# Where matmul operands lie in SBUF: three small constants in one tile, and a 368-byte filler

## The chip, the cores and the metric

The kernel runs on one core of a Trainium2 chip, as one launch. The metric is device time in microseconds, from the start of an execution to its end. Before the change the median of three runs is 2976.22 us (2974.38 to 2978.99). Five engines matter here: TensorE (PE in the profile; its weight loads are shown apart as PEld), VectorE (DVE), ScalarE (ACT), GpSimd (POOL), and SyncE (SP), whose queue issues the DMAs.

## The reference, cut to what matters

The reference takes `x` of 512 tokens by 1024 features through two stacks of two layers. All arithmetic is fp32.

- First stack, layer 0: RMS norm, dilated sliding-window attention (3 groups of 8 heads, head dimension 128, windows 128, 512, 2048 with dilations 1, 4, 16, a bias from a table of 32 buckets), output projection, norm, residual. Then a feed-forward with a causal convolution of width 3: `u = conv(h @ W_up)`, `(gelu(u[:, :3072]) * u[:, 3072:]) @ W_down`.
- First stack, layer 1: a gated linear recurrence (input projection, convolution of width 4, two block-diagonal gates, a scan over the tokens, output projection), then the same feed-forward.
- Second stack, two layers: three attentions side by side on one input projection (differential attention with a bias table, stick-breaking attention, latent attention with rotary positions), an output projection, attention over a memory of 256 rows, and a feed-forward `square(relu(h @ W1)) @ W2` of 4096.

Nearly all of the work is products of a 512 x 1024 activation with weights:

```
h = rms_norm(x, g)                 # 512 x 1024
u = h @ w_up                       # 1024 x 6144, feed-forward of the first stack
y = act(u) @ w_down                # 3072 x 1024
u = h @ w_ff1; y = relu(u)**2 @ w_ff2   # 1024 x 4096, 4096 x 1024, second stack
```

## The kernel before, in words

*Products in three terms.* Each fp32 operand of a large product is held as two fp32r tiles, high part and rest. `mm3` (lines 159 to 163) adds three TensorE products into one accumulator in PSUM: high by high (L161), high by rest (L162), rest by high (L163):

```
mm(out, sh, mh, start=first, stop=False)
mm(out, sh, ml, start=False, stop=False)
mm(out, sl, mh, start=False, stop=last)
```

The first operand (`sh`, `sl`) is the stationary one, 128 x 128, which a weight load brings into the array; the second (`mh`, `ml`) is the moving one, 128 x 512 in most cases.

*Which tile is which operand.* `up` (L253) computes 128 output features for all 512 tokens: the weight tile `w` is stationary, the transposed activation `hT` moves; 8 steps over the 1024 features make 24 products. `down` and `down_last` (L515 to L556) compute 128 tokens by 512 output features: an activation tile (`act`, in other stages `oT`, `gh`, `mo`) is stationary, `w` moves. `proj_tok` (L891) and the value projections of the first attention compute tokens by features too, with `hT` stationary and `w` moving; a part of the latter reads `hT` with a stride of four tokens. The recurrence's gates have `w` stationary and `xh` moving.

*Weights.* `load` (L138) brings 512 KB by DMA into one of three `raw` tiles. `cut` (L144) writes the high part on ACT (L148) and the rest on DVE (L149) into one of five `w` tiles of the pool `ws`; in `down_last` the second half of the columns takes its `w` tiles from a pool of the stage's own. Inside `w`, high part and rest lie 4096 bytes apart, steps of a product 512 bytes (stationary) or 2048 bytes (moving). Inside `hT` high part and rest lie 16384 bytes apart, and the steps are 2048 bytes.

*Order.* The program is unrolled. Stages follow one another in `build` (L1559): first attention, feed-forward, recurrence, feed-forward, then for each of two layers the mixed attentions, the memory attention and a feed-forward. Within a stage, generators are woven by hand (`weave`, `pipe`, the lists `START`, `UNITS`, `FILL`); Tile, the layer that the kernel is written in, gives each engine its order of instructions and all semaphores, and assigns SBUF addresses.

*Places.* SBUF pools lie one behind the other in the order in which they are opened; a tile's bytes per partition are rounded up to a multiple of 32. The constants come first, from byte 16512 (the bytes below hold a DMA buffer of 16384 bytes and four constants of 32 bytes each). Worked out from the sizes, the tiles of the kernel before begin here:

```
tile or pool                       first byte    modulo 512
ident (512 bytes)                       16512           128
ones (4 -> 32)                          17024           128
x (16384)                               17056           160
hT (32768)                              33440           160
eps (4 -> 32), mhalf (32)               66208           160, 192
raws (3 x 4096)                         66272           224
ws (5 x 8192)                           78560           224
nrm (5 x 4096)                         119520           224
tiny (4224 in all)                     140000           224
pool "lruc" (768), later pool "two"    144224           352
first attention, first feed-forward,
  recurrence: oT, act, xh, gh          144992            96
second feed-forward and second stack:
  act (behind "two", 6688 bytes)       150912           384
```

`lruc` (L1572) holds the recurrence's small vectors and is closed after stage 2; `two` (L1582) then takes its place and holds the bias table `tb2` of 32 bytes, a mask, the rotary table and the memory's keys and values. Tiles of the pools opened later in a stage (the `w` tiles of `down_last`, for one) follow from there: 96 in the recurrence, 352 in the first feed-forward, 128 in the second, 384 in the last two.

*The small tiles.* `ones`, `eps` and `mhalf` are written once by POOL (L108, L112, L114); `mhalf` is read by the power that makes each norm's factor (L202, on POOL), `eps` by a logarithm on ACT, `ones` by a scan on DVE. `tb` (L312) and `tb2` (L823) hold the two bias tables; each is filled by one DMA and read as stationary operand in `toeplitz` (L285). `tiny` holds the small per-token statistics, four buffers of each kind.

Of the kernel before, what the change touches and what calls it, by code (L numbers as in the profile page):

```python
# [9 lines left out]
F32 = mybir.dt.float32  # L10
# [10 lines left out]
P = 128  # L21
NT = S // P
KD = D // P
NEG = -1e30
EPS = 1e-6


def hbm(ap, offset, dims):
# [3 lines left out]
def pipe(gens):  # L32

    live = []
    for g in gens:
        if g is not None:
            live.append(g)
        live = [x for x in live if next(x, 0) is None]
        yield
    while live:  # L40
        live = [x for x in live if next(x, 0) is None]
        yield
# [30 lines left out]
def weave(*streams):  # L73
    for _ in woven(*streams):
        pass
# [17 lines left out]
class Net:  # L93
    def __init__(self, ctx, tc, a):
        self.ctx, self.tc, self.nc, self.a = ctx, tc, tc.nc, a
        nc = tc.nc
        pool = lambda name, bufs, **k: ctx.enter_context(tc.tile_pool(name=name, bufs=bufs, **k))
        self.const = pool("const", 1)
        self.raws = pool("raws", 3)
        self.ws = pool("ws", 5)  # L100
        self.nrm = pool("nrm", 2)
        self.tiny = pool("tiny", 4)
        self.ps = pool("ps", 8, space=PSUM)
        self.dram = pool("dram", 1, space=DRAM)
        self.ident = self.const.tile([P, P], F32, name="ident")
        make_identity(nc, self.ident)
        self.ones = self.const.tile([P, 1], F32, name="ones")
        nc.gpsimd.memset(self.ones, 1.0)  # L108
        self.x = self.const.tile([P, NT, D], F32, name="x")
        self.hT = self.const.tile([P, 2, KD, S], F32R, name="hT")  # L110
        self.eps = self.const.tile([P, 1], F32, name="eps")
        nc.gpsimd.memset(self.eps, EPS)  # L112
        self.mhalf = self.const.tile([P, 8], F32, name="mhalf")
        nc.gpsimd.memset(self.mhalf, -0.5)  # L114
        self.lnexp = False
        self.stage = 0
        self.act_norm = False
        self.n = 0
        self.last_gelu = None
# [56 lines left out]
    def rsqrt(self, ss, scale, shape, tag):  # L176
# [4 lines left out]
        if shape[0] <= (1 if self.lnexp else 4):  # L181
            nc.vector.tensor_scalar(v, ss, scale, EPS, op0=ALU.mult, op1=ALU.add)
            nc.gpsimd.tensor_tensor(y, v, self.mhalf[:, :shape[0]], op=ALU.pow)
        else:
            nc.scalar.activation(v, ss, AF.Ln, bias=self.eps, scale=scale)
            nc.vector.tensor_scalar(nm, ss, -0.5 * scale, -0.5 * EPS, op0=ALU.mult, op1=ALU.add)
            nc.scalar.activation(y, v, AF.Exp, scale=-0.5)
# [5 lines left out]
    def rms(self, hs, n=D):  # L193
# [4 lines left out]
        for i, h in enumerate(hs):  # L198
            nc.scalar.activation(scr[:, i * n // 2:(i + 1) * n // 2], h, AF.Square, scale=n ** -0.5,
                                 accum_out=ss[:, i:i + 1])  # L200
        nc.vector.tensor_scalar(ss[:, 2:3], ss[:, 0:1], ss[:, 1:2], EPS, op0=ALU.add, op1=ALU.add)
        nc.gpsimd.tensor_tensor(ss[:, 3:4], ss[:, 2:3], self.mhalf[:, :1], op=ALU.pow)  # L202
# [92 lines left out]
    def attn(self, l):  # L295
# [4 lines left out]
        with ExitStack() as cx:  # L300
            qks = cx.enter_context(self.tc.tile_pool(name="at_qk", bufs=4))
            oTs = cx.enter_context(self.tc.tile_pool(name="at_o", bufs=8))
            one = cx.enter_context(self.tc.tile_pool(name="at_c", bufs=1))
# [5 lines left out]
            LS = (383, 255, 255)  # L309

            def setup():
                tb = one.tile([33, 24], F32, name="tb")  # L312
                nc.sync.dma_start(tb[:32], a["rel_bias"])
                nc.vector.memset(tb[32:33], NEG)
                for g in range(3):
                    oh = self.nrm.tile([P, D], F32, tag=("gb", "xn", "xn")[g], name=self.nm("oh"))[:33, :LS[g]]
                    nc.sync.dma_start(oh, a[f"c_oh{g}"])
                    if g == 0:
                        yield
                    scr.append(self.dram.tile([P, 8, LS[g]], F32, name=f"tz{g}"))  # L320
                    yield from self.toeplitz(lambda h, g=g: tb[:, g * 8 + h:g * 8 + h + 1], oh, LS[g], 8, scr[g],
                                             (lambda: self.nrm.tile([P, D], F32, tag="scr", name=self.nm("fz"), bufs=1))
                                             if g else (lambda: qks.tile([P, D], F32, tag="qk", name=self.nm("fz"))),
                                             None if g else self.bank)
# [217 lines left out]

            self.act_norm = False
            tables = setup()
            start()
            self.act_norm = True
# [271 lines left out]
    def setup2(self, pool):  # L818

        a, nc = self.a, self.nc  # L820
        L = 639
        self.da_scr = self.dram.tile([P, 8, L], F32, name="da_scr")
        tb = pool.tile([32, 8], F32, name="tb2")  # L823
        nc.sync.dma_start(tb, a["rel_bias_2"])
        oh = self.nrm.tile([P, D], F32, tag="xn", name=self.nm("oh"))[:32, :L]
        nc.sync.dma_start(oh, a["c_ohda"])
        yield from self.toeplitz(lambda h: tb[:, h:h + 1], oh, L, 8, self.da_scr,
                                 lambda: self.nrm.tile([P, D], F32, tag="scr", name=self.nm("fz"), bufs=1))
        self.cmask = pool.tile([P, 512], F32, name="cmask")
        nc.gpsimd.memset(self.cmask, 0.0)  # L830
        nc.gpsimd.memset(self.cmask[0:64, 448:], NEG)
        self.rope = pool.tile([P, NT, 2, 16], F32, name="rope")
        nc.sync.dma_start(self.rope, a["c_rope"].rearrange("(t p) c f -> p t c f", p=P))
# [725 lines left out]
def build(tc, a, out, stages=range(10)):  # L1559
    gains = ["norm_mix_pre", "norm_ffn_pre"] * 2 + ["mix_norm_g_2", "memx_norm_g_2", "ffn_norm_g_2"] * 2  # L1560
    layer = [0, 0, 1, 1, 0, 0, 0, 1, 1, 1]
    with ExitStack() as ctx:
        net = Net(ctx, tc, a)
        net.out = out[0]
        net.next_g, net.next_gb = a[gains[stages[0]]][layer[stages[0]]], None
        if stages[0]:
            for t in range(NT):
                tc.nc.sync.dma_start(net.x[:, t], a["x"][0, t * P:(t + 1) * P])
            weave((pipe(net.after(t) for t in range(NT)), 1))
        two = None  # L1570
        early = ExitStack()
        lru_pool = early.enter_context(tc.tile_pool(name="lruc", bufs=1))  # L1572
        for n, s in enumerate(stages):
            net.gains = [a[gains[i]][layer[i]] for i in stages[n + 1:n + 3]] + [None, None]
            net.next_g, net.next_gb = net.gains[0], None
            l = layer[s]
            net.stage = s
            net.act_norm = s < 2
            if s > 2:
                early.close()  # L1580
            if s in (3, 6) or s > 3 and two is None:
                two = two or ctx.enter_context(tc.tile_pool(name="two", bufs=1))  # L1582
                fill = net.prep(0 if s < 6 else 1, two)
            if s in (4, 7):
                weave((fill, 1))
                if not net.lnexp:
                    net.lnexp_tables()
            if s == 0:
                net.attn(l)
            elif s == 2:  # L1590
                if not hasattr(net, "lru_c"):
                    weave((net.lru_setup(lru_pool), 1))
                net.lru(l)
            elif s < 4:
                net.ffn1(l, fill if s == 3 else net.lru_setup(lru_pool))
            elif s in (4, 7):
                net.mix(l)
            elif s in (6, 9):
                net.ffn2(l, fill if s == 6 else None)
        early.close()  # L1600
# [64 lines left out]
```

## Time and profile before

```
median of three runs                       2976.22 us
profiled execution                         2979.35 us
its span, first to last instruction        2977.6 us
granted TensorE clock, mean                0.998
PE busy / PEld busy                        2927.2 us (98%) / 2402.7 us (81%)
DVE / ACT / POOL busy                      1676.8 us (56%) / 1250.8 us (42%) / 169.3 us (6%)
TensorE products                           14210
DMA                                        287.35 MB, mean 97 GB/s
```

How to read it: busy time is the union of an engine's instructions. Matmuls are pipelined, and each one's end is modelled, so that it overlaps the start of the next; a PE that is busy all the time can still be shortened. What one product costs in a full stream is the distance from its start to the next one's, which the view in order of time shows (start in us, length in us, engine, line, operation, tiles). Names stand as out<-in, the inputs in alphabetical order and not in the order stationary, moving.

### The profile page before, as it was taken

Reading aid. Unit: us, or ns where it says so; the run is one execution under the profiler, and the core shown is the slowest. Engines: PE = TensorE matmul, PEld = TensorE weight load, DVE = VectorE, ACT = ScalarE, POOL = GpSimd, SP = SyncE. Lnnn points to the kernel's source line nnn. Section 1 sums busy time; section 2 is a strip of 40 time slices with the busy share of each in tenths; the row PEclk is TensorE's granted clock in tenths of the full one; section 3 lists DMA queues with packets and bytes.
Section 4 is the critical chain, followed back from the end, with each engine's and each line's share of the span. In section 5 each row is a group of like instructions: output and inputs, shape, how many; then the busy total and the mean of one; then the engine's idle time right before and its main releaser. Section 6 shows DMA issues by size and latency. Waiting matters only on the chain.

```text
span 2977.6 us, 37084 instructions
## 1 busy us (share of the span) xinstructions
PE 2927.2 (98%) x14210; PEld 2402.7 (81%) x14210; DVE 1676.8 (56%) x3182; ACT 1250.8 (42%) x2427; POOL 169.3 (6%) x257
## 2 busy tenths in 40 slices
PE   9999999999999999999999999999999999999999
PEld 6888888888888778777887877888887877888887
DVE  3234344646556876445558587745545578754443
ACT  4333333543334664433345467523223467532221
POOL 0000000000000311000002031000001022000000
PEclk9999999999999999999999999999999999999999
DMA  5332232323332232333343331233333332123322
GB/s 183 95 87 84 80 93 96 110 93 94 97 92 85 78 121 88 95 107 112 95 121 108 107 123 43 66 105 113 109 92 115 101 123 79 29 85 96 96 93 71
DMA packets 335924, 287.35 MB, mean 97 GB/s; under 512 B 14041, under 2 KB 272484, under 8 KB 335748
## 3 DMA queue, kind: packets, MB, share of 16 engines
q1 hardware_dynamic: 335748, 284.99, 31.2%
q8 instruction: 112, 1.84, 0.3%
q14 instruction: 64, 0.52, 0.1%
HBM read 272.34 MB, written 12.62 MB: 96 GB/s over the span
## 4 chain that ended last, share of the span: by engine, by line
PE 55%; DVE 7%; ACT 2%; issue 1%; POOL 1%; DMA 1%; POOLq 0%; ACTq 0%; DVEq 0%
PE acc L161 16%; PE acc L162 16%; PE acc L163 16%; PE acc L1073 1%; PE tr L212 1%; PE acc L1086 1%; DMA raw<-in_w_in_dram 1%; PE tr L928 1%; DVE w L149 1%; PE acc L1218 1%; PE acc L1412 0%; ACT w L148 0%; PE acc L1392 0%; DVE z L1130 0%; DVE lru_hs L773 0%
## 5 line engine op out<-in xcount | busy, mean ns | idle before, releaser
L149 DVE TENSOR_TENSOR w<-raw,w 128x1024 fp32r<-128x1024 f32 (+1 forms) x456 | 553.3, 1216 | 388.9 <-ACT w L148 386.6
L161 PE MATMUL acc<-hT,w 128*128 128x512 f32 (+1 forms) x1992 | 761.2, 383 | 0.2 <-ACT hT L167 0.2
L163 PE MATMUL acc<-hT,w 128*128 128x512 f32 (+1 forms) x1992 | 758.4, 381 | 2.9 <-DVE w L149 2.8
L162 PE MATMUL acc<-hT,w 128*128 128x512 f32 (+1 forms) x1992 | 759.0, 381 | 0.4 <-DVE hT L168 0.4
L148 ACT CAST w<-raw 128x1024 fp32r<-128x1024 f32 (+2 forms) x464 | 477.8, 1033 | 497.7 <-PE acc L163 426.7
L163 PEld LDWEIGHTS acc<-hT,w 128*128 128x128 f32 x1992 | 375.0, 188 | 82.8 <-DVE w L149 4.2
L161 PEld LDWEIGHTS acc<-hT,w 128*128 128x128 f32 x1992 | 374.7, 188 | 81.2 <-issue 2.6
L162 PEld LDWEIGHTS acc<-hT,w 128*128 128x128 f32 x1992 | 375.0, 188 | 78.9 <-DVE hT L168 1.1
L162 PE MATMUL acc<-w,act 128*128 128x512 f32 x896 | 355.8, 397 | 0.0
L161 PE MATMUL acc<-w,act 128*128 128x512 f32 x896 | 354.1, 396 | 0.3 <-ACT act L167 0.3
L163 PE MATMUL acc<-w,act 128*128 128x512 f32 x896 | 352.4, 394 | 0.0
L161 PE MATMUL acc<-w,hT 128*128 128x512 f32 (+2 forms) x768 | 286.2, 373 | 1.3 <-ACT w L148 1.3
L163 PE MATMUL acc<-w,hT 128*128 128x512 f32 (+2 forms) x768 | 276.2, 360 | 0.0
L162 PE MATMUL acc<-w,hT 128*128 128x512 f32 (+2 forms) x768 | 275.2, 358 | 0.0
L587 DVE SCALAR_TENSOR_TENSOR u<-acc,cw,u 128x511 f32<-128x511 f32 x192 | 143.6, 748 | 205.9 <-ACT u L585 202.7
L161 PEld LDWEIGHTS acc<-w,act 128*128 128x128 f32 x896 | 168.3, 188 | 43.2 <-ACT act L167 1.6
L163 PEld LDWEIGHTS acc<-w,act 128*128 128x128 f32 x896 | 168.3, 188 | 40.3 <-DVE act L168 0.6
L162 PEld LDWEIGHTS acc<-w,act 128*128 128x128 f32 x896 | 168.4, 188 | 38.9
L161 PEld LDWEIGHTS acc<-w,hT 128*128 128x128 f32 x768 | 161.4, 210 | 21.4 <-issue 2.4
L162 PEld LDWEIGHTS acc<-w,hT 128*128 128x128 f32 x768 | 161.7, 211 | 17.1 <-issue 2.4
L163 PEld LDWEIGHTS acc<-w,hT 128*128 128x128 f32 x768 | 161.3, 210 | 15.1
L585 ACT ACTIVATE u<-acc,cw 128x512 f32<-128x512 f32 x96 | 74.6, 777 | 219.8 <-PE acc L163 219.7
(381 smaller groups left out, 3312.2 us busy)
## 6 DMA issues: line engine op xcount, KB each, us to landing
raw<-in_w_ff_dram SPq DMA_DIRECT2D x128, 512.0 KB
raw<-in_ffn_w_up_dram SPq DMA_DIRECT2D x96, 512.0 KB
raw<-in_attn_w_qkv_dram SPq DMA_DIRECT2D x72, 512.0 KB
raw<-in_ffn_w_down_dram SPq DMA_DIRECT2D x48, 512.0 KB
raw<-in_w_in_dram SPq DMA_DIRECT2D x40, 512.0 KB
raw<-in_lru_w_in_dram SPq DMA_DIRECT2D x16, 512.0 KB
raw<-in_w_out_dram SPq DMA_DIRECT2D x16, 512.0 KB
x<-in_x_dram SPq DMA_DIRECT2D x8, 512.0 KB
```

Of the source, the lines that this page charges most:

```text
L148: nc.scalar.copy(w[:, 0], raw)
L149: (lo or nc.vector).tensor_sub(w[:, 1], raw, w[:, 0].bitcast(F32))
L161: mm(out, sh, mh, start=first, stop=False)
L162: mm(out, sh, ml, start=False, stop=False)
L163: mm(out, sl, mh, start=False, stop=last)
L212: nc.tensor.transpose(b[:, j * P:(j + 1) * P], src[:, k * P:(k + 1) * P], self.ident)
L585: nc.scalar.activation(u, b, AF.Identity, bias=cw[:, 3, j:j + 1], scale=cw[:, 2, j:j + 1])
L587: nc.vector.scalar_tensor_tensor(u[:, s:], b[:, :S - s], cw[:, i, j:j + 1], u[:, s:], op0=ALU.mult, op1=ALU.add)
L928: nc.tensor.transpose(b[:, j * P:(j + 1) * P], src[:, j * P:(j + 1) * P], self.ident)
L1073: nc.tensor.matmul(o[:, oc:oc + dv], pT[:, k * P:(k + 1) * P], v(k), start=(k == 0), stop=(k == i))
L1086: nc.tensor.matmul(b[:, :w], QZ[:, h, m, i * P:(i + 1) * P], kT[:, h, :w], start=True, stop=True)
L1218: nc.tensor.matmul(b[:, :w], MT[:96, i, 0, h], MT[:96, :i + 1, 1, h], start=True, stop=True)
```

## The change

`ones`, `eps` and `mhalf` become columns 0, 1 and 2 to 9 of one tile `small` of 128 columns (512 bytes), which lies between `ident` and `x`. The bias tables `tb` and `tb2` become columns 32 to 55 and 16 to 23 of `small`, and leave the pools `at_c` and `two`. A tile `place` of 368 bytes that no instruction uses is taken from `tiny`. No engine instruction is added or removed.

```diff
+TINY = 368
...
+        self.small = self.const.tile([P, P], F32, name="small")
+        self.ones, self.eps, self.mhalf = self.small[:, 0:1], self.small[:, 1:2], self.small[:, 2:10]
-        self.ones = self.const.tile([P, 1], F32, name="ones")
         nc.gpsimd.memset(self.ones, 1.0)
         self.x = self.const.tile([P, NT, D], F32, name="x")
         self.hT = self.const.tile([P, 2, KD, S], F32R, name="hT")
-        self.eps = self.const.tile([P, 1], F32, name="eps")
         nc.gpsimd.memset(self.eps, EPS)
-        self.mhalf = self.const.tile([P, 8], F32, name="mhalf")
         nc.gpsimd.memset(self.mhalf, -0.5)
...
-                tb = one.tile([33, 24], F32, name="tb")
+                tb = self.small[:33, 32:56]
...
-        tb = pool.tile([32, 8], F32, name="tb2")
+        tb = self.small[:32, 16:24]
...
+        net.tiny.tile([P, TINY // 4], F32, name="place", bufs=1)
         lru_pool = early.enter_context(tc.tile_pool(name="lruc", bufs=1))
```

## Rows read from the trace of the kernel before

**Rows 1.** Stretches: from:to, length, busy us (count) of PE, PEld, DVE, ACT, POOL; clock, DMA.
```profile
587.00:946.00 359.00, 359.00 (x1549) 288.86 (x1548) 202.47 (x284) 131.44 (x164) 0.00 (x0) 1.00 0.32 99
992.00:1150.00 158.00, 148.10 (x624) 117.39 (x623) 124.28 (x151) 101.66 (x154) 40.19 (x37) 0.97 0.30 89
```

**Rows 2.** PE groups by line and shape: count, busy us, mean ns, idle before.
```profile
L161 PE MATMUL acc<-hT,w 128*128 128x512 f32 x1720 | 686.4, 399 | 0.0
...
L161 PE MATMUL acc<-w,act 128*128 128x512 f32 x896 | 354.1, 396 | 0.3 <-ACT act L167 0.3
...
L161 PE MATMUL acc<-w,hT 128*128 128x512 f32 x512 | 210.0, 410 | 0.0
...
L161 PE MATMUL acc<-hT,w 128*128 128x256 f32 x272 | 75.1, 280 | 0.2 <-ACT hT L167 0.2
L161 PE MATMUL acc<-w,hT 128*128 128x256 f32 x192 | 55.6, 289 | 1.3 <-ACT w L148 1.3
```

**Rows 3.** PE in order of time (start us, length us), `up`, first and 28th start.
```profile
599.77 0.39 PE L161 MATMUL acc<-hT,w 128*128 128x512 f32 x1
...
606.07 0.40 PE L161 MATMUL acc<-hT,w 128*128 128x512 f32 x1
```

**Rows 4.** The same, `down` of the second feed-forward, first and 25th start.
```profile
1212.07 0.40 PE L161 MATMUL acc<-w,act 128*128 128x512 f32 x1
...
1217.67 0.40 PE L161 MATMUL acc<-w,act 128*128 128x512 f32 x1
```

**Rows 5.** The same, `down` of the first feed-forward, first and 28th start.
```profile
627.75 0.40 PE L161 MATMUL acc<-w,act 128*128 128x512 f32 x1
...
634.01 0.40 PE L161 MATMUL acc<-w,act 128*128 128x512 f32 x1
```

**Rows 6.** The same, token projection of the mixed attentions, first and tenth start.
```profile
1610.40 0.39 PE L161 MATMUL acc<-w,hT 128*128 128x512 f32 x1
...
1612.46 0.40 PE L161 MATMUL acc<-w,hT 128*128 128x512 f32 x1
```

**Rows 7.** The same, recurrence's `down_last`: twelve with `ws`, twelve with own weights.
```profile
1123.17 0.39 PE L161 MATMUL acc<-w,gh 128*128 128x512 f32 x1
...
1125.73 0.40 PE L163 MATMUL acc<-w,gh 128*128 128x512 f32 x1
...
1127.12 0.39 PE L163 MATMUL acc<-w,gh 128*128 128x512 f32 x1
...
1128.48 0.39 PE L163 MATMUL acc<-w,gh 128*128 128x512 f32 x1
```

**Rows 8.** The same, products of the memory's keys, sixth and last of twelve.
```profile
1481.54 0.39 PE L163 MATMUL acc<-w,mT 128*128 128x512 f32 x1
...
1482.90 0.39 PE L163 MATMUL acc<-w,mT 128*128 128x512 f32 x1
```

**Rows 9.** The same, second feed-forward's `down_last`, own weights, six starts apart.
```profile
1568.70 0.39 PE L163 MATMUL acc<-w,act 128*128 128x512 f32 x1
...
1570.06 0.39 PE L163 MATMUL acc<-w,act 128*128 128x512 f32 x1
```

**Rows 10.** The same, first attention, `hT` stationary with a stride, 18 starts apart.
```profile
93.28 0.41 PE L161 MATMUL acc<-w,hT 128*128 128x512 f32 x1
...
97.60 0.41 PE L161 MATMUL acc<-w,hT 128*128 128x512 f32 x1
```

**Rows 11.** ACT groups in 600 to 940 us, then in 1210 to 1550 us.
```profile
L585 ACT ACTIVATE u<-acc,cw 128x512 f32<-128x512 f32 x40 | 31.1, 777 | 86.7 <-PE acc L163 86.7
...
L585 ACT ACTIVATE u<-acc,cw 128x512 f32<-128x512 f32 x37 | 28.8, 778 | 105.7 <-PE acc L163 105.7
```

**Rows 12.** Start of the kernel in order of time, and a row of SP's waits.
```profile
0.80 0.39 SPq L313 DMA_DIRECT2D tb<-in_rel_bias_dram  x1
0.86 0.08 DVE L314 MEMSET tb<- 1x24 f32 x1 [0.86 <-PEq L1652]
...
SPq L824 <- PE acc L163: 22.4, 1, 22.4
```

## The prediction

> **What bounds the kernel now.** Read the table of stretches first: in the first feed-forward (587 to 946 us, one of four such stages) TensorE is busy in all 359 us, DVE in 202, and the DMA engines for a third of the time; even in the recurrent stage, where DVE has most to do, TensorE holds 148 of 158 us [rows 1]. So the end is set by how fast TensorE gets through its queue. Next come the groups by line and shape: the 128x512 products of the three lines of `mm3` (L161, L162, L163) are 3 x 1720 with `hT` moving and `w` stationary, 3 x 896 with `w` moving and `act` stationary, 3 x 512 with `w` moving and `hT` stationary [rows 2]. Their "mean ns" of about 399 overlaps the next instruction and is no price; what counts is the distance from start to start, and only the order of time shows it.
>
> That distance depends on where the two operands lie, and this is what the change touches. I took each product's two addresses modulo 512 from the tile sizes (the table in the section on the kernel) and read the start-to-start time of long unbroken runs:
> - moving at 160, stationary at 224 (all the `up` products): 27 starts in 6.30 us, 233.3 ns each [rows 3].
> - moving 224, stationary 384 (`down` of the later stages): 24 in 5.60 us, 233.3 ns [rows 4].
> - moving 224, stationary 96 (`down` of the first feed-forward): 27 in 6.26 us, 231.9 ns [rows 5].
> - moving 224, stationary 160 (token projections): 9 in 2.06 us, 228.9 ns [rows 6].
> - equal places: in one and the same `down_last` of the recurrent stage, the half whose weights are in `ws` (224 against 96) takes 11 starts in 2.56 us, 232.7 ns, and the next half, whose weights are in the stage's own pool (96 against 96), settles after six starts at 6 in 1.36 us, 226.7 ns [rows 7]. The memory keys' products (224 against 224) settle at the same 226.7 ns, 6 in 1.36 us [rows 8]. So do those at 128 against 384, a distance of 256: 6 in 1.36 us [rows 9].
>
> The same engines run beside both halves in rows 7, so place, not neighbours, makes the 6 ns. The slowest steady pitch in the trace is 240 ns, 18 starts in 4.32 us, where the stationary operand is read with a stride of four elements [rows 10].
>
> A rule of the Trainium skill speaks against all this. Its page "TensorE: Matmul & The Clock Gate", section "Step-by-step: what each phase is for", has TensorE read the moving operand and the weights through two independent ports, so that loading the next weights takes nothing from the running product. The same page's section "Back-to-back issue gap" gives N / 2.4 + 2.5 ns, 216 ns at 512 columns, wherever the operands lie. By that the change is worth nothing. Rows 7 disagree: 232.7 against 226.7 ns within three microseconds.
>
> **The change, part by part.** *The places.* `small` (512 bytes) in place of `ones`, `eps` and `mhalf` (32 bytes each, after rounding) lies before `x`, so `x`, `hT`, the weights and `nrm` all come to 128 modulo 512. `tiny` was 4224 bytes, 8 x 512 + 128; with the filler (368 rounds up to 384) it is 9 x 512, so the pools behind it begin at 128 again. The `lruc` pool (768 bytes) puts the tiles of the first attention, the first feed-forward and the recurrent stage at 384; pool `two` without `tb2` is 13 x 512, which puts those of the later stages at 128. Every `mm3` pair of long runs is then at distance 0 or 256, the two that ran at 226.7 ns. Terms, against 226.7 ns:
> - `up`, 5160 products, 233.3 to 226.7: 5160 x 6.6 = 34 us.
> - `down` at 384: three of the four feed-forwards, 2112 less the 144 already at a good distance: 1968 x 6.6 = 13 us. At 96: 528 x 5.2 = 3 us.
> - token projections: of 1536, 384 are the strided ones, which I leave at 240 (128 + 4 t is at no good distance); 1152 x 2.2 = 2.5 us.
> - the rest at 512 columns (`oT`, `gh`, `xh`, `mo`), some 480 products by about 5 ns: 2 us.
> - 256 columns: 1392 products, for which no row has an equal pair. Nothing, or half of what 512 columns gain: 0 to 4.6 us. I take 2.
>
> Together 57 us. Two things come off. A run needs six starts to settle, 1.39 us where 6 x 226.7 is 1.36 [rows 7]: 0.03 us a run. The feed-forwards hold about 6000 products in few long runs (the first of the four has 1549 instructions on TensorE [rows 1]) of the 10,800 in the five large groups [rows 2]; the other 4800 come in pieces of 12 to 24 between transposes and scores, so 200 to 400 runs, 6 to 12 us. I take 10. And in the recurrent stage TensorE is busy in 148 of 158 us, DVE in 124 [rows 1]: there, and around the attention's softmax, a quicker product partly waits for DVE. The savings there are about 6 us; I take 2 off. Left: 45 us.
>
> *What is late next.* In the feed-forward DVE would need 202 us in some 349 instead of 359 [rows 1], and the weights 99 GB/s become 102, so neither takes over.
>
> *Other engines on moved tiles.* The convolution's first step reads and writes a tile at 96 in the first feed-forward and at 384 in the second: 777 and 778 ns [rows 11]. I cost the moved tiles at nothing on ACT and DVE. A 1% loss or gain there would be hidden under a full TensorE.
>
> *Shared tile.* The memsets, the two bias tables' DMAs and the readers stay; only the tile is shared. Whether a DMA into columns 32 to 55 waits for the memsets of columns 0 to 9 depends on how finely waits are kept. In this kernel they follow regions: the memset of `tb`'s last row starts 0.06 us after its DMA was issued into the other rows, with no wait [rows 12]. So 0; if whole tiles counted, the first DMA would wait for memsets that end at about 1.1 us (0.3 us late on SP, and its `oh`, the first weights and `x` behind it), and the second table's DMA would hold one POOL power for a landing, about 2 us. Bounds 0 to 3 us. From the other side, `tb2`'s DMA held SP for 22.4 us on TensorE, because its memory was another pool's [rows 12]; queued behind it are the rotary table and the next weights. In `small` it need not wait, but `rope` still lies in that pool and takes the wait over. 0, at best 1 us.
>
> **Sum.** The profiled execution took 2979.35 us, 1.75 more than its span of 2977.6. 2979.35 - 45 = 2934. The median of the runs is 3.1 lower, 2976.22, so 2931 us. With no settling, no loss and the 256-column gain in full it is 57 + 2.6 + 1 = 61 us, 2915. If equal places give `up` only the 228.9 ns of rows 6, the terms are 5160 x 4.4 + 2496 x 3.8 less 12 = 20 us, 2956.
>
> **Rivals.**
> - *Only the products with moving `w` gain.* All the equal pairs that I could read have `w` as the moving operand (halves 4 KB apart); in `up` it is `hT`, whose halves lie 16 KB apart, and no row shows that at distance 0. Then the 34 us are missing: 45 - 34, and some 5 us less settling, is 16 us, 2960 us. Against it: the strides from k to k+1 are multiples of 512 in both forms, and rows 8 have the stationary layout of `up`.
> - *The filler does not count* (a tile that nothing uses is given no bytes). Then the pools behind `tiny` are 384 lower: `act` at distance 128 from `w`, where rows 5 show no gain, while `up` gains in full: 45 - 16 = 29 us, 2947 us. For it: nothing writes the tile.
> - *Nothing happens*: the pitch follows something else that differs between the halves of rows 7, such as the pool. 2976 us, within 6. Three stages with one number speak against it [rows 7 to 9]. The two ports of the Trainium skill's page, above, would give the same result.
> - *Slower*: weights and moving operand now start in the same place of the same 512 bytes, and in `up`, with its 16 KB halves, they meet instead of passing. Its pitch goes to the slowest steady one known, 240 ns: 5160 x 6.7 = 35 us more, less the 16 us that the other forms gain: +19, 2995 us. It decides from 236.4 ns in `up`, where 5160 x 3.1 = 16. Against it, no contiguous pair at distance 0 or 256 was slow.
>
> **How the numbers follow.** Forecast 0.70, only moving `w` 0.12, no filler 0.05, nothing 0.08, slower 0.05. Runs of one kernel here lie 0.15% apart, so 0.2% (6 us) is what a measurement can tell. Faster is 0.70 + 0.12 + 0.05 = 0.87, the same 0.08, slower 0.05. The range goes from the full gain, 2915, to the rival with moving `w`, 2960, and leaves out the last two cases and about half of that rival.
>
> **What would show it.** In order of time, `up` runs at 226.7 ns instead of 233.3 and `down` likewise; the four feed-forward stretches shorten by 9 us each, the second attention by about 2. TensorE stays full in them. The durations of ACT and DVE do not move. `up` at 233 with a faster `down` is the first rival; a run that keeps falling out of 226.7 within a long stretch, or a TensorE that begins to wait for the cut weights (DVE L149), makes the forecast too low.

## The result and the profile after

The changed kernel takes 2931.51 us (median of five runs, 2930.68 to 2933.84); the kernel before took 2976.57 us beside it (2974.38 to 2979.56). The ratio is 0.9851, with a 95% interval of [0.984, 0.9862]: 45 us less. 2931 was predicted.

The page of the changed kernel, its first lines (busy us, share of the span, instructions):

```profile
span 2929.0 us, 37083 instructions
...
PE 2876.2 (98%) x14210; PEld 2403.9 (82%) x14210; DVE 1675.7 (57%) x3182; ACT 1251.9 (43%) x2427; POOL 169.9 (6%) x257
```

PE lost 51.0 us of busy time; no other engine moved by more than 1.2 us, and every engine has the same count of instructions as before. (The lines of `mm3` are now L163 to L165.) The stretches that answer to [rows 1], the first feed-forward and the recurrent stage:

```profile
579.00:929.00 350.00, 350.00 (x1557) 289.86 (x1556) 203.10 (x285) 132.08 (x165) 0.00 (x0) 1.00 0.33 101
...
974.00:1130.00 156.00, 145.09 (x634) 117.83 (x633) 125.35 (x154) 103.07 (x153) 40.35 (x37) 0.98 0.31 91
```

The first is 9 us shorter and TensorE still full; the second 2 us shorter, with DVE's work within 1.1 us of before. Measured from its first 256-column `up` product to its last `down` product, each of the four feed-forwards is shorter: by 9.1, 9.1, 8.6 and 8.8 us in order of time. Then the order of time (start us, length us): `up` with 27 starts between its two rows, `down` of the second feed-forward with 21, `down_last` of the recurrence with 36, and the products with strided `hT` with 18:

```profile
589.95 0.39 PE L163 MATMUL acc<-hT,w 128*128 128x512 f32 x1
...
596.07 0.39 PE L163 MATMUL acc<-hT,w 128*128 128x512 f32 x1
...
1205.25 0.39 PE L163 MATMUL acc<-w,act 128*128 128x512 f32 x1
...
1210.01 0.39 PE L163 MATMUL acc<-w,act 128*128 128x512 f32 x1
...
1103.64 0.39 PE L163 MATMUL acc<-w,gh 128*128 128x512 f32 x1
...
1111.80 0.39 PE L163 MATMUL acc<-w,gh 128*128 128x512 f32 x1
...
90.81 0.40 PE L163 MATMUL acc<-w,hT 128*128 128x512 f32 x1
...
95.04 0.40 PE L163 MATMUL acc<-w,hT 128*128 128x512 f32 x1
```

`up`: 6.12 / 27 = 226.7 ns, where [rows 3] have 233.3. `down`: 4.76 / 21 = 226.7, where [rows 4] have 233.3. In `down_last` the two halves of [rows 7], 232.7 and 226.7, have become one run of 8.16 / 36 = 226.7. The strided products, 240 in [rows 10], are at 4.23 / 18 = 235.0, which I had not expected.

The 256-column products of `up` went the other way. Before, 33 starts apart, 3.75 / 33 = 113.6 ns:

```profile
574.93 0.28 PE L161 MATMUL acc<-hT,w 128*128 128x256 f32 x1
...
578.68 0.28 PE L161 MATMUL acc<-hT,w 128*128 128x256 f32 x1
```

After, 48 starts apart, 5.76 / 48 = 120.0 ns:

```profile
569.84 0.28 PE L165 MATMUL acc<-hT,w 128*128 128x256 f32 x1
...
575.60 0.28 PE L165 MATMUL acc<-hT,w 128*128 128x256 f32 x1
```

I summed the time from each product's start to the next one's, by kind of product, over both traces (the last product of the trace has no next one, so `down` counts 2687):

```
                                  products   before    after     change
up, 512 columns                       5160   1226.5   1193.4     -33.1
act stationary (down)                 2687    629.8    614.7     -15.1
hT stationary, contiguous             1152    279.7    278.6      -1.1
other 512-column pairs                 696    175.7    174.9      -0.8
hT stationary with a stride            384     93.2     91.6      -1.6
up, 256 columns                        816    102.8    105.7      +2.9
hT stationary, 256 columns             576     73.1     73.4      +0.3
transposes, scores, all else                                      -0.1
spans, us                                    2977.6   2929.0     -48.6
```

The profiled executions differ by 48.6 us, the medians by 45: the profiled one of before lay 3 us above its median.

The small edits, in SP's list of waits and in the rows of two single lines (duration ns min/median/max, first and last start):

```profile
SPq L835 <- PE acc L165: 22.2, 1, 22.2
...
L826 SPq DMA_DIRECT2D small<-in_rel_bias_dram x1: 333/333/333, 21.8 to 21.8; - x1
...
L587 ACT ACTIVATE u<-acc,cw x96: 761/781/786, 572.0 to 1531.1; 128x512 f32<-128x512 f32 x96
```

The second bias table's DMA now goes out at 21.8 us, and the rotary table's (L835) has taken over its wait: 22.2 us where [rows 12] have 22.4. ACT's convolution step takes 781 ns (the median of all 96), where [rows 11] have 777 and 778.

### The profile page after: what moved, and what is told of

It reads as the page before. It is cut to its first block, busy times and chain, and to the rows that moved or that the text cites. A ratio compares the mean times of both kernels' runs of the same rounds, so it can differ in the third digit from the quotient of the medians.

```text
span 2929.0 us, 37083 instructions
## 1 busy us (share of the span) xinstructions
PE 2876.2 (98%) x14210; PEld 2403.9 (82%) x14210; DVE 1675.7 (57%) x3182; ACT 1251.9 (43%) x2427; POOL 169.9 (6%) x257
## 4 chain that ended last, share of the span: by engine, by line
PE 54%; DVE 7%; ACT 2%; issue 1%; POOL 1%; DMA 1%; SPq 0%; POOLq 0%; ACTq 0%; DVEq 0%
PE acc L163 16%; PE acc L165 16%; PE acc L164 16%; PE acc L1075 1%; PE acc L1088 1%; PE tr L214 1%; DVE w L151 1%; PE tr L930 1%; DMA raw<-in_w_in_dram 1%; PE acc L1220 1%; PE acc L1414 1%; PE acc L1394 0%; DVE z L1132 0%; PE tr L287 0%; ACT w L150 0%
## 5 line engine op out<-in xcount | busy, mean ns | idle before, releaser
L163 PE MATMUL acc<-hT,w 128*128 128x512 f32 (+1 forms) x1992 | 752.5, 378 | 0.2 <-ACT hT L169 0.2
L165 PE MATMUL acc<-hT,w 128*128 128x512 f32 (+1 forms) x1992 | 749.2, 376 | 3.3 <-DVE w L151 3.3
L164 PE MATMUL acc<-hT,w 128*128 128x512 f32 (+1 forms) x1992 | 750.1, 377 | 0.5 <-DVE hT L170 0.5
L165 PEld LDWEIGHTS acc<-hT,w 128*128 128x128 f32 x1992 | 375.4, 188 | 71.9 <-DVE w L151 4.2
L163 PEld LDWEIGHTS acc<-hT,w 128*128 128x128 f32 x1992 | 374.9, 189 | 70.4 <-issue 2.6
L163 PE MATMUL acc<-w,act 128*128 128x512 f32 x896 | 349.6, 391 | 1.3 <-ACT act L169 1.2
L164 PE MATMUL acc<-w,act 128*128 128x512 f32 x896 | 349.0, 390 | 0.0
L165 PE MATMUL acc<-w,act 128*128 128x512 f32 x896 | 348.7, 390 | 0.0
L163 PE MATMUL acc<-w,hT 128*128 128x512 f32 (+2 forms) x768 | 285.6, 372 | 1.2 <-ACT w L150 1.2
L165 PE MATMUL acc<-w,hT 128*128 128x512 f32 (+2 forms) x768 | 274.9, 358 | 0.0
L163 PEld LDWEIGHTS acc<-w,act 128*128 128x128 f32 x896 | 168.2, 188 | 37.5 <-ACT act L169 2.7
L165 PEld LDWEIGHTS acc<-w,act 128*128 128x128 f32 x896 | 168.1, 188 | 35.4 <-DVE act L170 0.6
L163 PEld LDWEIGHTS acc<-w,hT 128*128 128x128 f32 x768 | 161.6, 210 | 21.3 <-issue 2.4
L165 PEld LDWEIGHTS acc<-w,hT 128*128 128x128 f32 x768 | 161.5, 210 | 14.9
```

## The experiments

**Each distance by itself.** This kernel leaves the network out and issues 59 runs of 48 products, back to back, whose operands lie at a chosen distance. Distance is the stationary operand's address less the moving one's; `d` counts elements of 4 bytes:

```diff
+st = lambda h, e=0: W[:, h * 1024 + k * 128 + d + p + e:h * 1024 + k * 128 + d + p + e + 128]
+mv = lambda h, e=0: X[:, h * 4096 + q * 512 + p + e:h * 4096 + q * 512 + p + e + n]
+ops = [(st(0), mv(0)), (st(0), mv(1)), (st(1), mv(0))]
```

> Leaves out the whole network: 55 runs of 48 three-term products on two tiles, only the place of the stationary operand against the moving one (and its width) differs. Theory (the pitch is set by the distance of the two operands modulo 512): at 512 columns the steady pitch is 226.7 ns at distance 0 and 256, about 229 at -64, 232 to 233.5 at +64, 160 and -128, and so on in between; moving both operands together by 64 to 448 bytes leaves 226.7. Rival (the pool or the stage made the difference): one pitch for all distances. Second rival (the absolute place of one operand): the runs with both moved together differ. At 256 columns distance 0 is slower than +64, about 120 against 113 ns, as the changed kernel shows. With the distance alternating, the product whose own weights are at distance 0 but the next weights at 128 bytes tells which of the two counts: if it is the load of the next weights under the running product, 'next' runs at 226.7 and 'own' at 230 or more; if its own, the other way round.

It took 588.48 us in its one execution. Its rows in order of time follow (start us, length us of the 48 together). The pitch of a run is the time from one start to the next, about the run's length less one product, divided by 47; it is settled when the first starts of the run, some ten as a rule, are past:

```profile
48.05 11.36 PE L63 MATMUL segac<-X,W 128*128 128x512 f32 x48
...
70.49 11.32 PE L63 MATMUL segae<-X,W 128*128 128x512 f32 x48
...
92.85 11.16 PE L63 MATMUL segag<-X,W 128*128 128x512 f32 x48
...
115.04 11.05 PE L63 MATMUL segai<-X,W 128*128 128x512 f32 x48
...
204.10 5.91 PE L63 MATMUL segba<-X,W 128*128 128x256 f32 x48
...
215.53 5.82 PE L63 MATMUL segbc<-X,W 128*128 128x256 f32 x48
...
316.87 11.08 PE L63 MATMUL segcc<-X,W 128*128 128x512 f32 x48
...
427.25 11.13 PE L63 MATMUL segcm<-X,W 128*128 128x512 f32 x48
438.21 11.20 PE L63 MATMUL segcn<-X,W 128*128 128x512 f32 x48
449.25 11.44 PE L63 MATMUL segco<-W,X 128*128 128x512 f32 x48
...
471.81 11.65 PE L63 MATMUL segda<-W,X 128*128 128x512 f32 x48
```

The first four are distances 64, 128, 192 and 256: (11.36 - 0.39) / 47 = 233.4 ns, 232.6, 229.1, 226.8. Then 256 columns at 0 and 64 (120 and 118), both operands moved together by 192 bytes (227.4 with settling), the two runs described below, and the strided stationary operand at 0 and 128. Settled, the table is:

```
distance modulo 256 (bytes)    0      32     64     96     128    160    192    224
512 columns, ns              226.7  233.3  233.3  234.5  232.3  233.3  228.9  233.3
256 columns, ns              120.0  118.4  117.8  117.3  118.7  120.0  117.8  117.8
```

Distances 256 to 480 repeat 0 to 224, so the period is 256 bytes. The kernel before fits in closely: 64 in [rows 3], 160 in [rows 4], 128 in [rows 5] and 192 in [rows 6] gave 233.3, 233.3, 231.9 and 228.9 ns. Even 4 bytes apart cost (232.4). Moved together, by 64 to 448 bytes, every pair settles at 226.7. With a strided stationary operand the pitch is 235.0 at 0 and 256 and 240.0 at 128 and 384. The strided products of the network went from distance 192, which these runs leave out, to 0, and show the same two values. At 256 columns equal places are at the slow end, level with 160. Two runs were to tell which stationary operand counts: with a product's own pair at distance 0 and the next one's at 128 the pitch is 228.3, the other way round 230.0. Both count, and the question stays open.

**Without the filler.** Undoes one line, which moves all pools behind `tiny` by 384 bytes and leaves `up` at distance 0:

```diff
-        net.tiny.tile([P, TINY // 4], F32, name="place", bufs=1)
```

> The change without the filler tile: weights, hT and x at 128 modulo 512, the activations behind the small pool at 0 and 256, distance 128 from the weights. Theory: up keeps its 226.7 ns, down runs at 232 to 233.5, so 13 + 3 + 2 us come back: 2948 us, between 2944 and 2952. Rival (the shared tile and the earlier DMA of the second bias table make the gain): 2931 us, no loss.

2948.19 us beside 2975.44 for the kernel before, ratio 0.9902 [0.9887, 0.9917]. In order of time `up` and `down`, 27 starts between the rows of each:

```profile
595.93 0.39 PE L165 MATMUL acc<-hT,w 128*128 128x512 f32 x1
...
602.05 0.39 PE L165 MATMUL acc<-hT,w 128*128 128x512 f32 x1
...
1207.93 0.39 PE L163 MATMUL acc<-w,act 128*128 128x512 f32 x1
...
1214.21 0.39 PE L163 MATMUL acc<-w,act 128*128 128x512 f32 x1
```

226.7 ns and 232.6 ns: `up` gains, `down` does not. In sum `down` takes 628.5 us, against 629.8 in the kernel before. The filler is worth about 17 us (2948.19 - 2931.51).

**Only the stationary activations moved.** The constants stay as before; only the pools behind `tiny` move, so that `act` comes to the place of `w` and `up` keeps its distance of 64:

```diff
+        pool.tile([P, 120], F32, name="place2")
         tb = pool.tile([32, 8], F32, name="tb2")
...
+        net.tiny.tile([P, 96], F32, name="place", bufs=1)
```

> The kernel before with two fillers alone (384 bytes in the small pool, 480 in the pool of the second stack): activations at 480 and 224, distance 256 and 0 from the weights, hT left at 160, distance 64. Theory: down at 226.7 ns, up at 233.3: 16 us faster than before less 1 to 3 for settling at each change between up and down: 2960 to 2963 us. Rival (equal places of all tiles are wanted, not of pairs): 2976 us.

2957.61 us beside 2975.44, ratio 0.9935 [0.9921, 0.995]. `up` and `down` again, 27 starts each:

```profile
595.93 0.40 PE L163 MATMUL acc<-hT,w 128*128 128x512 f32 x1
...
602.23 0.39 PE L163 MATMUL acc<-hT,w 128*128 128x512 f32 x1
...
1215.01 0.39 PE L161 MATMUL acc<-w,act 128*128 128x512 f32 x1
...
1221.13 0.39 PE L161 MATMUL acc<-w,act 128*128 128x512 f32 x1
```

233.3 and 226.7 ns: the mirror image. `down` takes 614.8 us in sum, 15.0 less than before. The run gains 18 us by the medians, a little more than expected, and the kernel without the filler gains 27: together the 45 of the whole change.

**The shared tile with the old places.** All edits of the change except the filler, and unused tiles that put every large tile back where it lay before:

```diff
+        self.const.tile([P, 8], F32, name="place1")
...
+        self.const.tile([P, 16], F32, name="place2")
...
+                one.tile([P, 24], F32, name="place3")
...
+        pool.tile([P, 8], F32, name="place4")
...
-        net.tiny.tile([P, TINY // 4], F32, name="place", bufs=1)
```

> The shared tile and the moved bias tables with fillers that put every other tile back at its old place modulo 512. Theory: nothing but the places matters, 2976 us, within 0.2%. Rival (the 22.4 us that the second bias table's DMA held SP were worth something, or false waits on the shared tile cost something): 1 to 3 us to either side, or more.

2977.61 us, ratio 1.0005 [0.9996, 1.0015]. TensorE's row of the page:

```profile
PE 2925.9 (98%) x14210; PEld 2401.8 (81%) x14210; DVE 1676.1 (56%) x3182; ACT 1251.0 (42%) x2427; POOL 172.0 (6%) x257
```

Sharing and the earlier DMA show no gain: by the interval they are worth between 1 us gained and 4.5 us lost. So the gain is place.

**Everything moved by 96 bytes.** The kernel before with one unused tile ahead of all others; distances kept:

```diff
+        self.const.tile([P, 24], F32, name="place")
```

> The kernel before with a filler of 96 bytes ahead of everything: every tile moves by 96 bytes, all distances stay. Theory (distance alone counts): 2976 us, within 0.2%. Rival (the absolute place modulo 64, 128 or 256 counts; the tiles at 160 and 224 go to 256 and 320): a difference of more than 6 us.

2974.82 us, ratio 0.9995 [0.9985, 1.0005]. A common shift of 96 bytes changes nothing outside the interval: the distance counts, not the place.

**Widths and what came before.** The kernel of the first experiment, with narrower stationary operands, other moving widths, and single products put ahead of a run. It leaves the network out too, and was executed once (540.94 us):

```diff
+            for w in sep:
+                nc.tensor.matmul(z[:, :w], W[:, :P], X[:, :w], start=True, stop=True)
...
+                st = lambda h: W[:, h * 1024 + k * 128 + d:h * 1024 + k * 128 + d + m]
```

> Leaves out the whole network: 60 runs of 48 three-term products; first with stationary operands of 128, 96, 64 and 32 columns at distances 0, 64 and 128 under 512 moving columns, then 448 to 128 moving columns, then 256 and 512 columns behind eight different openings of one or two odd products. The first pitch run gave 226.7, 173.3 and 120.0 ns at distance 0 for 512, 384 and 256 moving columns, which is 213.3, 160 and 106.7 (columns at 2.4 GHz) plus 13.3 ns each. Theory A (the 13.3 ns are what the next weight load takes from the running product, and a bad distance adds to it): with fewer stationary columns the addition shrinks in proportion, 128 columns 13.3, 64 columns about 6.7, 32 about 3.3, and the difference between distances shrinks with it. Theory B (13.3 ns are a fixed cost of a product): 226.7 for all widths at distance 0. Theory C on the history: at 256 columns and distance 64 the same operands can settle at 113.3 or at 118, by what ran before; at distance 0 and at 512 columns there is one pitch for all openings.

Rows in order of time; the stationary operand is 128, 96, 96, 64 and 32 columns wide, at distances 64, 0, 128, 0 and 0; the last two are 256 columns at distance 64 after one product of 128 and after one of 384 columns:

```profile
34.87 11.36 PE L55 MATMUL segab<-X,W 128*128 128x512 f32 x48
...
57.22 11.21 PE L55 MATMUL segad<-X,W 128*96 128x512 f32 x48
...
79.23 11.04 PE L55 MATMUL segaf<-X,W 128*96 128x512 f32 x48
90.11 11.20 PE L55 MATMUL segag<-X,W 128*64 128x512 f32 x48
...
123.33 11.27 PE L55 MATMUL segaj<-X,W 128*32 128x512 f32 x48
...
229.27 5.87 PE L55 MATMUL segbh<-X,W 128*128 128x256 f32 x48
...
235.15 5.61 PE L55 MATMUL segbi<-X,W 128*128 128x256 f32 x48
```

Settled at distances 0, 64 and 128: 96 columns wide 230.0, 228.3, 226.7; 64 wide 230.0, 232.8, 229.3; 32 wide 231.7, 231.7, 231.0. A narrower weight load does not lessen the cost; it changes which distance is good. So it is not simply the share of time in which the load reads, and of these four widths only 128 columns have their 226.7 at distance 0. At 512 columns eight openings changed nothing (233.3 and 226.7). At 256 columns and distance 64 there are two settled pitches, 113.3 in six openings and 117.8 in two; the last two rows are one of each ((5.87 - 0.28) / 47 = 118.9, (5.61 - 0.28) / 47 = 113.4). At distance 0 it is 120.0 after all eight. The same eight openings at a distance of 96 bytes gave three settled pitches: 117.3 after four, 118.7 after three, 120.0 after one. So the entries for 256 columns at 64 and 96 in the table above hold for what ran before them there. The 113.6 of the kernel before was the good one of two. Other moving widths: 384 columns take 173.3 ns at distances 0 and 192, 176.0 at 128 and 176.7 at 64 (first experiment); 448 take 202.7 at 0 and 202.2 at 64; 320 take 146.7, and both 192 and 128 take 111.7, at 0 and at 64 alike.

**Split weights 64 bytes further.** A try at a better version: the weights of the split `up` products lie 64 bytes into larger slots. To make room, `small` has 256 bytes, `tiny` three buffers of a kind, the filler 160 bytes:

```diff
-TINY = 368
+TINY = 160
...
-        self.tiny = pool("tiny", 4)
+        self.tiny = pool("tiny", 3)
...
+            w = self.ws.tile([P, 2112], F32R, tag=tag, name=self.nm("w"))
+            w = w[:, off:off + 2 * a * b].rearrange("p (w a b) -> p w a b", w=2, a=a)
...
-                    ws = [self.w_in(Win, j * P) for j in js]
+                    ws = [self.w_in(Win, j * P, off=16) for j in js]
```

> The changed kernel, with the weights of the split up products (256 columns, about 860 of them) 64 bytes further in their slots of 8448 bytes, so their distance to hT is 64 modulo 256; all 512-column pairs stay at 0 modulo 256 (filler 160 bytes, small tile 256 bytes, tiny with three buffers instead of four). Theory A (distance sets the pitch of 256 columns too, 113.3 or 117.8 ns at 64 against 120.0 at 0): 860 x 2.2 to 860 x 6.7 = 2 to 6 us below the same layout without the offset, up at 256 columns about 100 to 104 us in sum instead of 105.7. So 2926 to 2930 if three buffers cost nothing. Theory B (the 256-column loss seen after the change came from the neighbours in time, not from the distance): no difference to the layout without the offset, 2931 both.

> The same layout (slots of 8448 bytes, filler 160 bytes, small tile 256 bytes, tiny with three buffers) without the offset: the control for the run before. Both theories: the time of the changed kernel, 2931 within 2; if the third tiny buffer matters, some microseconds more, and then in the run with the offset too.

2947.85 us and, for the control, 2950.63. Both missed what was expected, because I had sized the filler wrongly by 128 bytes. The 4224 bytes of `tiny` do not shrink to three quarters (3168): 512 of them belong to kinds of tile with two or eight buffers of their own, not four, which the edit leaves alone, so 3296 are left. `act` lay at distance 128, and `down` was back at 232.3 ns and 628.7 and 629.1 us in sum. So both ran again with a filler of 32 bytes:

```diff
-TINY = 160
+TINY = 32
```

> As e7 (split up products at distance 64 modulo 256), but with a filler of 32 bytes instead of 160. In e7 and e8 the filler had put act at 256 modulo 512, at distance 128 from w (down at 232.3 ns each, the 14 us that both lost against the changed kernel); 128 bytes less put it at distance 0. Theory A (places explain e7 and e8 whole): down 226.8, down in sum about 614.7 instead of 628.7, the rest of the 512-column pairs 3 us less: 2947.9 - 17 = 2931 - 2 to 3 for the split products = 2928 to 2931. Theory B (three tiny buffers cost the 17 us): 2945 to 2948 still.

> The control for the run before: same layout, no offset, every pair at 0 modulo 256. Theory A: 2931 within 2, and 2 to 3 us above the run with the offset. Theory B: 2949.

2931.26 us, ratio 0.9854 [0.9839, 0.9868], and 2934.5, ratio 0.9863 [0.9846, 0.9879]. `down` is back at 614.4 us in both. With the offset the split products, 48 starts apart, go at 5.66 / 48 = 117.9 ns:

```profile
569.71 0.28 PE L167 MATMUL acc<-hT,w 128*128 128x256 f32 x1
...
575.37 0.28 PE L167 MATMUL acc<-hT,w 128*128 128x256 f32 x1
```

In sum they take 103.9 us against 105.7 in the control. The runs show 3.2 us between the two, but their intervals overlap; 1.8 us of it is the split products. The control is 3 us above the changed kernel at the same steady pitch (227.15 ns in `up` in both, 1197.1 against 1193.4 us in sum), so it waits more somewhere. Three buffers alone do not explain it: the run with the offset has three as well and takes 1194.1 us in `up`, and the kernel without the filler has four and takes 1198.0. What it waits for stays open. The version ends level with the changed kernel, 2931.26 against 2931.51.

## Why the prediction was right, step by step

- *`up`, 34 us*: 33.1, and its steady pitch is the predicted one. *`down`, 16 us*: 15.1. These two terms are the change. The other 512-column pairs gave 1.9 where 4.5 stood: their runs are short (of 81 with `hT` stationary, all but six have 24 products or fewer), and the `hT`-stationary ones average 228.7 ns instead of 226.7.
- *Settling, 10 us*: too much. Over the pairs under 300 ns, the excess over 226.7 is 2.4 us in `up` (5024 by 0.48), 0.5 in `down`, 2.1 with `hT` stationary and 0.8 in the rest: 5.8 us, and these are within the measured changes above, not beside them.
- *256 columns, 2 us gained*: the wrong sign, 3.2 lost. I carried the rule of 512 columns over without a row for it. Equal places are the slow end there (120.0), and the kernel before ran at the better of two pitches for its distance.
- *Strided, nothing*: 1.6 gained, 235.0 ns instead of 240.0. I had ruled it out because the stride reaches places at no good distance; the distance of its start counts all the same (235.0 at 0 and 256, 240.0 at 128 and 384 in the runs of products alone).
- *Waiting for DVE, 2 us off 6*: 5.4 came. From the last `down` product before it to the first 256-column `up` product of the next feed-forward, the recurrent stage is 3.0 us shorter and each of the two mixed-attention stages 1.2.
- *The shared tile, the DMA, ACT and DVE at nothing*: so it was. The wait passed to the rotary table as written, and ACT's 781 ns left TensorE full in the feed-forward.
- The errors met: the forecast came to 45 us for the profiled execution, and the spans differ by 48.6, so it was 3.6 us short there: settling was over-counted, the 256 columns had the wrong sign. The medians differ by 45 because the profiled execution of before lay 3 us above its median. The hit to within 1 us is in part luck; the mechanism is not, since the terms that carry it were measured singly, by the runs without the filler and with the activations alone.
- The rivals: *only moving `w`* predicted 233 for `up`, which is at 226.7; the run in which only `down` gains took 2957.61, near that rival's 2960. *The filler does not count* named 2947, which the kernel without it took (2948.19). *Slower* falls with the same rows. *Nothing happens* falls: the runs of products alone go from 226.7 to 234.5 ns by the distance of the operands. With it falls the one pitch for all places that the prediction drew from the Trainium skill, page "TensorE: Matmul & The Clock Gate". Its section "Step-by-step: what each phase is for" says that loading the next weights takes no read bandwidth from the running product, through a port of its own. These runs do not show what is contended, but they show that the place of the weights counts. Its section "Back-to-back issue gap" gives the 216 ns at 512 columns for an isolated product, and about 131 for a stream of weight loads and products; no stream of 512 columns here settled below 226.7.

## What to carry to other kernels

When a stream of products is unbroken, read its start-to-start time per pair of tiles before costing anything else; where it differs between pairs of one shape, take the two addresses modulo 256. Unused bytes between pools are a cheap edit (one line here), but compute the places of all pairs after it, since every later pool moves (128 bytes wrong cost 16 to 17 us here, 2950.63 against 2934.5 and 2947.85 against 2931.26). Measure each width by itself: the best distance for 512 columns was at the slow end for 256.

## What the runs showed of the hardware

- The pitch of 128x128 by 128x512 fp32r products, weights loaded for each, depends on the distance of the operands (stationary less moving) with a period of 256 bytes: 226.7 ns at 0, 228.9 at 192, 230.7 to 234.5 at all others tried.
- A pair 4 bytes apart is already slow (232.4 ns). The absolute place made no difference in any common shift tried (64 to 448 bytes at distance 0, and 96 bytes for the whole kernel).
- At 256 columns and distance 64 there are two settled pitches, 113.3 and 117.8 ns, and at distance 96 three, 117.3, 118.7 and 120.0, chosen by what ran before; at distance 0 there was one (120.0), and at 512 columns one (233.3 at distance 64, 226.7 at 0).
- With 96 stationary columns 128 bytes are best (226.7) and 0 the worst of three (230.0). What is contended stays open: neither a cost in proportion to the load nor a fixed one fits.
